# An mLSTM decoder step: gate rows by chunk and head, one empty step ahead of the first gate products, and decode state steps in program order

## The chip, the cores and the metric

The kernel runs on one core of one Trainium2 chip. A core has five engines with queues of their own: TensorE (PE, with its weight loads PEld), VectorE (DVE), ScalarE (ACT), GpSimd (POOL) and SyncE (SP). Each works its own instructions strictly in order and waits on the others through semaphores. The metric is the device time of one execution in microseconds (us).

## What is computed

One layer of a hybrid decoder works on a prompt of 1024 tokens and on 8 single decode tokens. Of the reference, what matters here is the mLSTM gate arithmetic, chunk by chunk (128 tokens, 8 chunks, 4 heads), with `ig` the input gate and `lf` the log forget gate:

```python
b = jnp.cumsum(lf, axis=1).transpose(0, 2, 1)
...
g = b + m[:, :, None]
m_t = jnp.maximum(g, jnp.max(D, axis=-1))
...
ginter = jnp.exp(g - m_t)
...
decay = jnp.exp(b[:, :, -1:] - b + igh - mL[:, :, None])
carry_scale = jnp.exp(b[:, :, -1] + m - mL)
```

`m` is the running maximum that is carried from chunk to chunk. The other two parts that the change touches are the gates of the RG-LRU group (two 64 x 64 products per block of channels, a sigmoid each) and, for each decode token and head, the update of the 256 x 256 state `C = f C + k v`, of which `q C` is then taken.

## The kernel before, in words

**The stages.** First the 1024 rows of x are normalised, transposed and split into pieces (to about 95 us). Then 13 units of the input projection follow (`UNITS`, units 1 to 13; unit 0 is done in the first stage). Each unit is seven products, numbered 0 to 6; a product is two parts, and each part is a run of 12 (q, k, x, y, z units) or 24 (v and o units) matmuls in groups of three (lines 64 to 66). I write "product (2,3) after 5" for the place behind the fifth matmul of product 3 of unit 2. After the units come the chunks of the mLSTM with the output projection in between (from about 690 us), and a short end.

**What runs beside the products.** After each part, `pop_bg` runs what has come due: `late` callbacks, then one step of the queue `bg` (two in units 1 and 13), one of `rgq` (RG-LRU), and in every second or third part one of `dcq` (decode state). The steps of `bg` begin with the generator `gates()` (line 567). Each `yield` in it ends a step. After it comes `rd_open`, which gives the gates' memory to the RG-LRU and decode tiles.

**The order on each engine.** The program is traced in the order of this Python code. A list scheduler then sets each engine's order ahead of time: by its own model of times it takes, in order of tracing, the first instruction that it believes ready. So an instruction that is ready early moves forward, and one that is not ready yet is put behind later matmuls. On the chip the order is fixed: if the model was too hopeful, the engine stands and waits. A place in the middle of a part, such as "(2,3) after 5", therefore marks an instruction that the scheduler put where it had just become ready, without slack.

**`gates()` before.** Parameters are loaded and transposed (L591), a chain of small operations on `gx` (128 x 72) makes the log forget gates (L597 to L602). Sixteen transposes (L630) turn gates into rows of [4 heads, 1024 tokens]; DVE copies them (L631), runs two scans over 1024 elements (L635 running maximum, L636 cumulative sum restarted at each chunk by a mask), and five further passes over [4, 1024] (L639, L642, L654, L656; ACT takes L655 and L657). They land in `stk`, four groups of 4 rows at partitions 0, 32, 64 and 96, and eight transposes (L664) turn `stk` back into columns [128, chunk x head].

**RG-LRU halves.** `rg_half(j, b)` is eight steps: `conv1` (L766, L768), `conv2` (L772, ACT copies L776), `lows` (L783, writes the low parts into `xh` and `xl`), `gate_a` and `gate_b` (the gate products L789), `decay`, `scan`, `outs`.

**Decode state.** For each head and token, `token(b)`: ACT scales the state tile `Cb` (L935), DVE adds k v in two halves (L937, with the broadcast row `vbc` that SP loads at L908), POOL stores it (L939). For every second token, two parts later, four small products (L956) read a pair of states. `Cb` has four buffers, loaded by SP at L914.

Of the kernel before, what the change touches and what calls it, by code (L numbers as in the profile page):

```python
# [9 lines left out]
F32 = mybir.dt.float32  # L10
# [7 lines left out]
P = 128  # L18
# [31 lines left out]
def hymba_kernel(  # L50
# [79 lines left out]
    cs_b = const([P, NH, NCH], "cs_b")  # L130
# [440 lines left out]
    def gates():  # L571
# [49 lines left out]
        stq(s_m, dm[0:1])  # L621
        yield

        rows = fp.tile([NH, 2, T], F32, tag="rows0", name="rows0")
        lfr, igr = rows[:, 0, :], rows[:, 1, :]
        for half in range(2):
            for src, dst in ((lf, lfr), (gs, igr)):
                pr = ps("s" if dst is lfr else "qp", [NH, 512])
                for q in range(4):
                    TE.transpose(pr[:, q * P:(q + 1) * P], src[:, half * 4 + q, 0:NH], idF)  # L630
                (A.copy if dst is igr else V.tensor_copy)(dst[:, half * 512:(half + 1) * 512], pr)  # L631
            yield
        rows1 = fp.tile([NH, 2, T], F32, tag="rows1", name="rows1")
        mr, br = rows1[:, 0, :], rows1[:, 1, :]
        V.tensor_tensor_scan(mr, lfr, igr, 0.0, op0=ALU.add, op1=ALU.max)  # L635
        V.tensor_tensor_scan(br, msk, lfr, 0.0, op0=ALU.mult, op1=ALU.add)  # L636
        yield
        al = lfr
        V.tensor_tensor(al, br, mr, op=ALU.subtract)  # L639
        ld(d_alpha, al)  # L640
        stq(p_m[0, 0].rearrange("(h o) -> h o", o=1), mr[:, T - 1:T])
        V.tensor_tensor(br, igr, br, op=ALU.subtract)  # L642
        c3 = lambda t: t.rearrange("p (c l) -> p c l", l=L)
        sm = fp.tile([NH, 3, NCH], F32, tag="gsm", name="gsm")
        mpv, aL, csr = sm[:, 0], sm[:, 1], sm[:, 2]
        G.memset(mpv, 0.0)
        V.tensor_copy(mpv[:, 1:NCH], c3(mr)[:, 0:NCH - 1, L - 1])
        V.tensor_copy(aL, c3(al)[:, :, L - 1])
        V.tensor_tensor(csr, aL, mpv, op=ALU.add)
        A.activation(csr, csr, AF.Exp)  # L650
        ld(d_cs, csr)
        ld(cs_b, d_cs.partition_broadcast(P))
        yield
        V.tensor_tensor(c3(stk[0:4]), c3(al), mpv.unsqueeze(2).to_broadcast([NH, NCH, L]), op=ALU.add)  # L654
        A.copy(stk[32:36], br)  # L655
        V.tensor_tensor(c3(stk[64:68]), c3(br), aL.unsqueeze(2).to_broadcast([NH, NCH, L]), op=ALU.add)  # L656
        A.mul(stk[96:100], mr, -1.0)  # L657
        for _ in range(5):
            yield
        for half in range(2):  # L660
            pk = ps(("s", "qp")[half], [P, 4, P])
            for q in range(4):
                c = half * 4 + q
                TE.transpose(pk[:, q, :], stk[:, c * P:(c + 1) * P], idF)  # L664
            s = slice(half * 4, half * 4 + 4)
            V.tensor_copy(be_t[:, s, :], pk[:, :, 32:36])
            A.activation(gi_t[:, s, :], pk[:, :, 0:4], AF.Exp)
            A.activation(de_t[:, s, :], pk[:, :, 64:68], AF.Exp)
            A.activation(em_t[:, s, :], pk[:, :, 96:100], AF.Exp)
            yield  # L670
# [77 lines left out]
    def rg_half(j, b):  # L748
# [70 lines left out]
        def outs():  # L819
# [96 lines left out]
    def decode_steps(h):  # L916
# [13 lines left out]
        def token(b):  # L930
            i = h * NB + b

            def f():
                vb_, C = ds_.pop(("v", i)), ds_["C", i]
                A.mul(C, C, dGI[:, b, h:h + 1])  # L935
                for kb in range(2):
                    V.scalar_tensor_tensor(C[:, kb, :], vb_, st["kw"][:, kb, b:b + 1], C[:, kb, :],  # L937
                                           op0=ALU.mult, op1=ALU.add)
# [144 lines left out]
    def w_load(n):  # L1083
        if n < 4 * NCH:
            c, h = n // 4, n % 4
            Ws[n] = mx["p"].tile([P, L], F32, tag="W", name="W", bufs=3)
            ld(Ws[n], d_alpha[h:h + 1, c * L:(c + 1) * L].rearrange("o t -> (o t)").partition_broadcast(P))

    sos = {}
    zt = {}  # L1090
# [87 lines left out]
    def m_b(n):  # L1178
# [8 lines left out]
        pv = ps("tr", [P, 258])  # L1187
        mm3(pv, d["ph"], d["pl"], *mx["v"], True, True)
        for kb in range(2):
            V.scalar_tensor_tensor(mx["Cf"][h][:, kb, :], mx["Cf"][h][:, kb, :], cs_b[:, h, c:c + 1], kvs[kb],  # L1190
                                   op0=ALU.mult, op1=ALU.add)
        V.tensor_tensor(hh, pv[:, 0:257], hh, op=ALU.add)
        if c == NCH - 1:
# [394 lines left out]
```

## Time and profile before

| what | us |
| --- | --- |
| three runs | 941.11, 940.55, 938.7 |
| their median | 940.55 |
| the profiled execution | 939.56 |
| its span, first to last instruction | 937.8 |
| TensorE busy in the span | 918.5 |

The profiled execution's time is 1.76 us more than its span, and 0.99 us less than the median of the three runs. How to read the views: a group row gives line, engine, operation, output and inputs, shape, count, then busy us and mean ns, then the idle time of that engine just before and what ended it. A row of the timeline gives start, duration, engine, line, and in brackets the idle time before it with its releaser. Matmuls overlap: their starts are about 0.23 us apart while each lasts 0.39 us. A row of the view of stretches gives busy time and count of each engine, then the granted TensorE clock, the DMA share and GB/s.

### The profile page before, as it was taken

Reading aid. Unit: us, or ns where it says so; the run is one execution under the profiler, and the core shown is the slowest. Engines: PE = TensorE matmul, PEld = TensorE weight load, DVE = VectorE, ACT = ScalarE, POOL = GpSimd, SP = SyncE. Lnnn points to the kernel's source line nnn. Section 1 sums busy time; section 2 is a strip of 40 time slices with the busy share of each in tenths; the row PEclk is TensorE's granted clock in tenths of the full one; section 3 lists DMA queues with packets and bytes.
Section 4 is the critical chain, followed back from the end, with each engine's and each line's share of the span. In section 5 each row is a group of like instructions: output and inputs, shape, how many; then the busy total and the mean of one; then the engine's idle time right before and its main releaser. Section 6 shows DMA issues by size and latency. Waiting matters only on the chain.

```text
span 937.8 us, 15396 instructions
## 1 busy us (share of the span) xinstructions
PE 918.5 (98%) x5350; PEld 760.6 (81%) x5350; DVE 712.1 (76%) x1465; ACT 590.5 (63%) x1054; POOL 145.6 (16%) x259
## 2 busy tenths in 40 slices
PE   9999989999999999999999999999999999999997
PEld 7897767777787987787789898876578888888886
DVE  7775898989798877988797866668857677667654
ACT  7654457778677757778578774465746466456542
POOL 1111112112212122211122211010111000000110
PEclk9999999999999999999999999999999999999999
DMA  6611457356746464545557363435973563565351
GB/s 197 208 41 44 135 157 264 106 177 203 242 145 209 158 207 164 180 128 196 183 196 242 130 197 107 152 115 181 298 228 118 168 189 116 149 188 162 102 102 46
DMA packets 131383, 153.19 MB, mean 163 GB/s; under 512 B 15816, under 2 KB 110056, under 8 KB 131298
## 3 DMA queue, kind: packets, MB, share of 16 engines
q1 hardware_dynamic: 113578, 96.34, 34.0%
q0 software_dynamic: 17728, 55.87, 16.6%
q8 instruction: 42, 0.69, 0.3%
q14 instruction: 35, 0.29, 0.1%
HBM read 100.59 MB, written 51.65 MB: 162 GB/s over the span
## 4 chain that ended last, share of the span: by engine, by line
PE 82%; DVE 6%; DMA 4%; issue 3%; ACT 2%; SPq 1%; POOL 0%; DVEq 0%; ACTq 0%; POOLq 0%
PE ps_o L64 14%; PE ps_o L66 13%; PE ps_o L65 13%; PE ps_kv L64 9%; PE ps_kv L65 9%; PE ps_kv L66 9%; PE ps_tr L236 2%; PE ps_s L1129 2%; DMA oraw<-in_w_out_dram 1%; DVE wl L71 1%; PE ps_qp L956 1%; PE ps_qp L65 1%; PE ps_qp L64 1%; PE ps_qp L66 1%; PE ps_s L1131 1%
## 5 line engine op out<-in xcount | busy, mean ns | idle before, releaser
L70 ACT CAST wh<-raw 128x1024 fp32r<-128x1024 f32 x91 | 95.4, 1049 | 60.9 <-PE ps_o L65 23.9
L71 DVE TENSOR_TENSOR wl<-raw,wh 128x1024 fp32r<-128x1024 f32 x91 | 110.9, 1219 | 27.2 <-ACT wh L70 17.9
L64 PE MATMUL ps_kv<-cb_hi,wh 128*128 128x512 f32 x320 | 128.0, 400 | 2.0 <-ACT wh L70 1.6
L66 PE MATMUL ps_kv<-cb_hi,wl 128*128 128x512 f32 x320 | 125.3, 392 | 0.0
L65 PE MATMUL ps_kv<-cb_lo,wh 128*128 128x512 f32 x320 | 125.2, 391 | 0.0
L64 PE MATMUL ps_o<-cb_hi,wh 128*128 128x512 f32 x240 | 95.1, 396 | 0.5 <-ACT wh L70 0.5
L66 PE MATMUL ps_o<-cb_hi,wl 128*128 128x512 f32 x240 | 93.8, 392 | 0.0
L65 PE MATMUL ps_o<-cb_lo,wh 128*128 128x512 f32 x240 | 93.6, 390 | 0.0
L64 PEld LDWEIGHTS ps_kv<-cb_hi,wh 128*128 128x128 f32 x320 | 60.1, 188 | 23.8 <-issue 3.0
L65 PEld LDWEIGHTS ps_kv<-cb_lo,wh 128*128 128x128 f32 x320 | 60.2, 188 | 13.3 <-issue 1.7
L66 PEld LDWEIGHTS ps_kv<-cb_hi,wl 128*128 128x128 f32 x320 | 60.1, 188 | 13.0
L64 PE MATMUL ps_kv<-wh,cb_hi 128*128 128x256 f32 x192 | 55.4, 288 | 0.0
L64 PEld LDWEIGHTS ps_o<-cb_hi,wh 128*128 128x128 f32 x240 | 45.1, 188 | 12.3 <-issue 2.5
L65 PE MATMUL ps_kv<-wl,cb_hi 128*128 128x256 f32 x192 | 54.3, 283 | 0.0
L66 PE MATMUL ps_kv<-wh,cb_lo 128*128 128x256 f32 x192 | 54.3, 283 | 0.0
L66 PEld LDWEIGHTS ps_o<-cb_hi,wl 128*128 128x128 f32 x240 | 45.1, 188 | 10.6 <-DVE pf L1138 0.8
L64 PE MATMUL ps_o<-wo,rh 128*128 128x512 f32 (+1 forms) x136 | 53.4, 393 | 0.0
L65 PEld LDWEIGHTS ps_o<-cb_lo,wh 128*128 128x128 f32 x240 | 45.1, 188 | 10.0 <-issue 0.8
L64 PE MATMUL ps_o<-wo,mh 128*128 128x512 f32 (+1 forms) x136 | 52.8, 389 | 0.0
L66 PE MATMUL ps_o<-wo,ml 128*128 128x512 f32 (+1 forms) x136 | 51.7, 381 | 0.0
L66 PE MATMUL ps_o<-wo,rl 128*128 128x512 f32 (+1 forms) x136 | 51.7, 381 | 0.0
L65 PE MATMUL ps_o<-wo,rh 128*128 128x512 f32 (+1 forms) x136 | 51.6, 379 | 0.0
(481 smaller groups left out, 2530.4 us busy)
## 6 DMA issues: line engine op xcount, KB each, us to landing
raw<-in_w_in_dram SPq DMA_DIRECT2D x55, 512.0 KB
Cb<-in_state_mlstm_C_dram SPq DMA_DIRECT2D x32, 256.0 KB
out_dram<-Cb POOLq DMA_DIRECT2D x32, 256.0 KB, 4.6
qk<-d_qk SPq DMA_DIRECT2D x32, 256.0 KB
oraw<-in_w_out_dram SPq DMA_DIRECT2D x16, 512.0 KB
d_qk<-s POOLq DMA_DIRECT2D x24, 256.0 KB, 3.9
d_x<-s POOLq DMA_DIRECT2D x16, 256.0 KB, 2.6
zsr<-d_y SPq DMA_DIRECT2D x16, 256.0 KB
```

The lines of the kernel that those rows point to most:

```text
L64: TE.matmul(out, ah, bh, start=first, stop=False, skip_group_check=True)
L65: TE.matmul(out, ah, bl, start=False, stop=False, skip_group_check=True)
L66: TE.matmul(out, al, bh, start=False, stop=last, skip_group_check=True)
L70: A.copy(hi, src)
L71: V.tensor_tensor(lo, src, hi.bitcast(F32), op=ALU.subtract)
L236: TE.matmul(pz[32 * g:32 * g + 32, :], hnd[:, NB * k:NB * k + 32], raws[u, k // 4][:, k % 4, :], start=k < 4, stop=k >= 4, skip_group_chec ...
L956: TE.matmul(pq[32 * g:32 * g + n, 0:256], q, ds_["C", h * NB + bb][:, kb, :], start=b == 1, stop=b == NB - 1, skip_group_check=True)
L1129: TE.matmul(S, qk[:, 2 + kb, :], qk[:, kb, :], start=kb == 0, stop=kb == 1)
L1131: TE.transpose(kn[:, kb * P:(kb + 1) * P], qk[:, 2 + kb, :], idF)
```

## The change

Three edits. In `gates()`, rows are now 32 (chunk and head) by 128 tokens: two transposes instead of sixteen, scans over 128 elements in 32 rows side by side, a small product (`hsel`, `ends`) that brings the chunk ends to [4, 8], an 8-element scan over chunks, a second small product (`mix`) that brings the carried maximum back to 32 rows, the same passes over [32, 128], and one transpose of `stk` instead of eight. The number of yields stays: 15 steps. In `rg_half` an empty step stands ahead of `gate_a` for b = 0 of j = 0 and 1, so all later RG-LRU steps come one, then two parts later. In `token`, the ACT operation and both DVE operations get an order edge behind the instruction traced just before them on their engine: they can no longer move forward past it.

```diff
-    d_alpha = dram.tile([NH, T], F32, name="d_alpha")
-    d_cs = dram.tile([NH, NCH], F32, name="d_cs")
+    d_alpha = dram.tile([NCH * NH, L], F32, name="d_alpha")
+    d_cs = dram.tile([NCH, NH], F32, name="d_cs")
...
-        stk = fp.tile([P, T], F32, tag="stk", name="stk")
-        msk = fp.tile([NH, T], F32, tag="msk", name="msk")
-        G.memset(msk, 1.0)
-        G.memset(msk.rearrange("p (c l) -> p c l", l=L)[:, :, 0:1], 0.0)
-        G.memset(stk, 0.0)
+        stk = fp.tile([P, L], F32, tag="stk", name="stk")
...
+        G.memset(mo, 0.0)
+        G.tensor_copy(igc.rearrange("p (c h) -> p c h", h=NH), gs[:, :, 0:4])
...
-        for half in range(2):
-            for src, dst in ((lf, lfr), (gs, igr)):
-                pr = ps("s" if dst is lfr else "qp", [NH, 512])
-                for q in range(4):
-                    TE.transpose(pr[:, q * P:(q + 1) * P], src[:, half * 4 + q, 0:NH], idF)
-                (A.copy if dst is igr else V.tensor_copy)(dst[:, half * 512:(half + 1) * 512], pr)
-            yield
...
-        V.tensor_tensor_scan(mr, lfr, igr, 0.0, op0=ALU.add, op1=ALU.max)
-        V.tensor_tensor_scan(br, msk, lfr, 0.0, op0=ALU.mult, op1=ALU.add)
+        V.tensor_reduce(hsel, idc.rearrange("p c h -> p h c"), axis=mybir.AxisListType.X, op=ALU.add)
+        V.tensor_reduce(csel, idc, axis=mybir.AxisListType.X, op=ALU.add)
+        yield
+        yield
...
+        TE.transpose(pr[:, 0, :], lg[:, 0:32], idF)
+        TE.transpose(pr[:, 1, :], igc, idF)
+        A.copy(rows[:, 0:2, :], pr)
+        V.tensor_tensor_scan(ml_, lfr, igr, -1e30, op0=ALU.add, op1=ALU.max)
+        V.tensor_tensor_scan(br, ones[0:CH, :], lfr, 0.0, op0=ALU.mult, op1=ALU.add)
...
+        V.tensor_scalar(ends[:, 0], csel, br[:, L - 1:L], None, op0=ALU.mult)
+        V.tensor_scalar(ends[:, 1], csel, ml_[:, L - 1:L], None, op0=ALU.mult)
+        yield
+        yield
+        yield
...
+        TE.matmul(pe.rearrange("p a c -> p (a c)"), hsel, ends.rearrange("p a c -> p (a c)"), start=True, stop=True)
...
+        V.tensor_copy(be, pe)
+        V.tensor_tensor_scan(mo[:, 1:9], be[:, 0], be[:, 1], 0.0, op0=ALU.add, op1=ALU.max)
...
+        V.tensor_tensor(mix, mo[:, 0:8].unsqueeze(2).to_broadcast([NH, NCH, NH]),
+                        idF[0:NH, 0:NH].unsqueeze(1).to_broadcast([NH, NCH, NH]), op=ALU.mult)
+        yield
+        yield
...
+        TE.matmul(pm, mix.rearrange("p c h -> p (c h)"), ones[0:NH, 0:1], start=True, stop=True)
...
+        V.tensor_copy(mi, pm)
+        V.scalar_tensor_tensor(mr, br, mi, ml_, op0=ALU.add, op1=ALU.max)
         V.tensor_tensor(al, br, mr, op=ALU.subtract)
+        V.tensor_tensor(br, igr, br, op=ALU.subtract)
         ld(d_alpha, al)
...
+        A.copy(stk[32:64], br)
+        A.mul(stk[96:128], mr, -1.0)
+        V.tensor_scalar(stk[0:32], al, mi, None, op0=ALU.add)
+        V.tensor_scalar(stk[64:96], br, aL, None, op0=ALU.add)
+        A.activation(mp[:, 1:2], aL, AF.Exp, bias=mi)
...
+        pk = ps("qp", [P, 4, CH])
+        TE.transpose(pk.rearrange("p g n -> p (g n)"), stk, idF)
...
-        return [conv1, conv2, lows, gate_a, gate_b, decay, scan, outs]
+        wait = [lambda: None] * (b == 0 and j < 2)
+        return [conv1, conv2, lows, *wait, gate_a, gate_b, decay, scan, outs]
...
-                A.mul(C, C, dGI[:, b, h:h + 1])
+                tc.keep_in_program_order(A.mul(C, C, dGI[:, b, h:h + 1]))
                 for kb in range(2):
-                    V.scalar_tensor_tensor(C[:, kb, :], vb_, st["kw"][:, kb, b:b + 1], C[:, kb, :],
-                                           op0=ALU.mult, op1=ALU.add)
+                    tc.keep_in_program_order(V.scalar_tensor_tensor(C[:, kb, :], vb_, st["kw"][:, kb, b:b + 1], C[:, kb, :],
+                                                                    op0=ALU.mult, op1=ALU.add))
```

The rest of the diff follows the new layout: the load of `W` reads row n of `d_alpha`, and `cs_b` is indexed by chunk, then head.

**What the built program shows of the order.** On TensorE the two new transposes stand at (1,6) after 2 (the sixteen of before stood in six groups between the first stage and (1,6) after 3), the two small products at (1,6) after 14 and after 18, the `stk` transpose behind (1,6) among the decode products of the next unit's weights (before: eight at (2,0) after 17). The first gate products L789 stand at (2,2) after 24 and (2,3) after 12 (before: (2,3) after 5 and after 6). The later pair that stood at (3,3) after 13 now stands at (3,4) after 12, the end of a part. Of the 16 groups of L956, five are now split, the second state's two products standing further back, in the middle of a part: (4,3) after 18 and 20, (5,5) after 21 and 23, (6,1) after 25 and 28, (8,5) after 17 and 19, (9,1) after 13 and 14; before, all 16 stood together at ends of parts. L789 stands in the middle of a part at (3,0) after 17 and (6,0) after 36, and between decode products behind (5,6). The first products of the mLSTM chunks (L1129) begin at the end of (11,6) instead of (11,5); from product (13,0) on, the order is that of before but for one place. TensorE has 5037 instructions before and 5018 after.

More of the change, by code (lines that the diff above doesn't have):

```diff
@@ L580, in gates @@
         ld(m0b, st_m[0].partition_broadcast(P))
-        stk = fp.tile([P, T], F32, tag="stk", name="stk")
-        msk = fp.tile([NH, T], F32, tag="msk", name="msk")
-        G.memset(msk, 1.0)
-        G.memset(msk.rearrange("p (c l) -> p c l", l=L)[:, :, 0:1], 0.0)
-        G.memset(stk, 0.0)
+        CH = NCH * NH
+        stk = fp.tile([P, L], F32, tag="stk", name="stk")
+        igc = fp.tile([P, CH], F32, tag="igc", name="igc")
+        mo = fp.tile([NH, 12], F32, tag="mo", name="mo")
+        G.memset(mo, 0.0)
+        G.tensor_copy(igc.rearrange("p (c h) -> p c h", h=NH), gs[:, :, 0:4])
+        idc = idF[0:CH, 0:CH].rearrange("p (c h) -> p c h", h=NH)
+        hsel = fp.tile([CH, NH], F32, tag="hsel", name="hsel")
+        csel = fp.tile([CH, NCH], F32, tag="csel", name="csel")
         dgb = fp.tile([P, NB, 8], F32, tag="dgb", name="dgb")
@@ new lines, in gates @@
+        rows = fp.tile([CH, 6, L], F32, tag="rows", name="rows")
+        lfr, igr, ml_, br, mr, al = (rows[:, n, :] for n in range(6))
+        pr = ps("s", [CH, 2, L])
+        TE.transpose(pr[:, 0, :], lg[:, 0:32], idF)
[3 more added lines that the diff above has]
+        V.tensor_tensor_scan(br, ones[0:CH, :], lfr, 0.0, op0=ALU.mult, op1=ALU.add)
+        ends = fp.tile([CH, 2, NCH], F32, tag="ends", name="ends")
@@ new lines, in gates @@
+        V.tensor_scalar(ends[:, 0], csel, br[:, L - 1:L], None, op0=ALU.mult)
[3 more added lines that the diff above has]
+        yield
+        pe = ps("qp", [NH, 2, NCH])
+        TE.matmul(pe.rearrange("p a c -> p (a c)"), hsel, ends.rearrange("p a c -> p (a c)"), start=True, stop=True)
+        be = fp.tile([NH, 2, NCH], F32, tag="be", name="be")
+        V.tensor_copy(be, pe)
+        V.tensor_tensor_scan(mo[:, 1:9], be[:, 0], be[:, 1], 0.0, op0=ALU.add, op1=ALU.max)
@@ new lines, in gates @@
+        mix = fp.tile([NH, NCH, NH], F32, tag="mix", name="mix")
+        V.tensor_tensor(mix, mo[:, 0:8].unsqueeze(2).to_broadcast([NH, NCH, NH]),
+                        idF[0:NH, 0:NH].unsqueeze(1).to_broadcast([NH, NCH, NH]), op=ALU.mult)
+        yield
+        yield
+        pm = ps("s", [CH, 1])
+        TE.matmul(pm, mix.rearrange("p c h -> p (c h)"), ones[0:NH, 0:1], start=True, stop=True)
+        mp = fp.tile([CH, 2], F32, tag="mp", name="mp")
+        mi, aL = mp[:, 0:1], al[:, L - 1:L]
@@ L646, in gates @@
[L646 to L651, printed above, removed]
+        stq(p_m[0, 0].rearrange("(h o) -> h o", o=1), mr[CH - NH:CH, L - 1:L])
+        A.copy(stk[32:64], br)
+        A.mul(stk[96:128], mr, -1.0)
+        V.tensor_scalar(stk[0:32], al, mi, None, op0=ALU.add)
+        V.tensor_scalar(stk[64:96], br, aL, None, op0=ALU.add)
@@ L652, in gates @@
+        A.activation(mp[:, 1:2], aL, AF.Exp, bias=mi)
+        ld(d_cs.rearrange("c h -> (c h)").rearrange("(p o) -> p o", o=1), mp[:, 1:2])
         ld(cs_b, d_cs.partition_broadcast(P))
         yield
[L654 to L670, printed above, removed]
+        yield
@@ L671, in gates @@
+        yield
+        pk = ps("qp", [P, 4, CH])
+        TE.transpose(pk.rearrange("p g n -> p (g n)"), stk, idF)
+        flat = lambda t: t.rearrange("p c h -> p (c h)")
+        V.tensor_copy(flat(be_t), pk[:, 1, :])
+        A.activation(flat(gi_t), pk[:, 0, :], AF.Exp)
+        A.activation(flat(de_t), pk[:, 2, :], AF.Exp)
+        A.activation(flat(em_t), pk[:, 3, :], AF.Exp)
+        yield
         ids = idF.rearrange("p (a g m) -> p a g m", a=2, g=2)
@@ L1086, in w_load @@
             Ws[n] = mx["p"].tile([P, L], F32, tag="W", name="W", bufs=3)
-            ld(Ws[n], d_alpha[h:h + 1, c * L:(c + 1) * L].rearrange("o t -> (o t)").partition_broadcast(P))
+            ld(Ws[n], d_alpha[n:n + 1, :].rearrange("o t -> (o t)").partition_broadcast(P))
     sos = {}
```

14 lines of the change are left out of this document (2 added, 12 removed).

## The prediction

> **What bounds the kernel now.** I read the page first, then TensorE's waits, then the view of stretches around those waits.
>
> ```profile
> span 937.8 us, 15396 instructions
> ...
> PE 918.5 (98%) x5350; PEld 760.6 (81%) x5350; DVE 712.1 (76%) x1465; ACT 590.5 (63%) x1054; POOL 145.6 (16%) x259
> ...
> PE 82%; DVE 6%; DMA 4%; issue 3%; ACT 2%; SPq 1%; POOL 0%; DVEq 0%; ACTq 0%; POOLq 0%
> ```
>
> TensorE works 918.5 of 937.8 us and holds 82% of the chain that ended last. So a change is worth what it takes from TensorE's own work, plus what it takes from or adds to TensorE's 19.3 us of idle time; relief elsewhere counts only through these two. The waits of TensorE, as wait, releaser, us in total, times, longest:
>
> ```profile
> PE ps_tr L1269 <- DMA oraw<-in_w_out_dram: 2.4, 2, 1.4
> PE ps_s L789 <- DVE xh L783: 2.0, 2, 1.5
> PE ps_s L664 <- DVE stk L656: 1.7, 1, 1.7
> PE ps_kv L64 <- ACT wh L70: 1.6, 1, 1.6
> ...
> PE ps_s L630 <- DVE gx L602: 0.3, 1, 0.3
> ```
>
> Three of them belong to what is changed: L630 and L664 to the gates, L789 to the first gate products of the RG-LRU. All three end with DVE. The stretch around the gates, all instructions first, then those on the tile `rows` alone:
>
> ```profile
> 100.00:125.00 25.00, 23.07 (x115) 16.84 (x115) 24.67 (x55) 11.27 (x19) 3.79 (x7) 1.00 0.28 96
> ```
> ```profile
> 100.00:125.00 25.00, 10.70 (x10) 2.10 (x2) 0.53 (x1) 1.00 0.28 96
> ```
>
> DVE (third number of the first row) is busy 24.67 of 25 us: here it is the bound, and TensorE loses 1.93 us. Of this DVE work 10.70 us, ten operations, are passes over [4, 1024] rows.
>
> **The change, part by part.**
>
> *TensorE's own work.* What a group of four transposes costs, and a single one, is read from the starts of the matmuls around them:
>
> ```profile
> 110.92 0.39 PE L66 MATMUL ps_kv<-cb_hi,wl 128*128 128x512 f32 x1
> 111.21 0.60 PE L630 MATMUL ps_s<-idF,gx 128*4 128x128 f32 x4
> 111.57 0.47 PE L64 MATMUL ps_kv<-cb_hi,wh 128*128 128x512 f32 x1
> 111.88 0.39 PE L65 MATMUL ps_kv<-cb_lo,wh 128*128 128x512 f32 x1
> ```
> ```profile
> 80.68 0.40 PE L66 MATMUL ps_kv<-cb_hi,wl 128*128 128x512 f32 x1
> 80.91 0.28 PE L630 MATMUL ps_qp<-idF,gs 128*4 128x128 f32 x1
> 80.94 0.47 PE L64 MATMUL ps_o<-cb_hi,wh 128*128 128x512 f32 x1
> 81.26 0.39 PE L65 MATMUL ps_o<-cb_lo,wh 128*128 128x512 f32 x1
> ```
> ```profile
> 138.24 0.39 PE L65 MATMUL ps_o<-cb_lo,wh 128*128 128x512 f32 x1
> 138.47 0.39 PE L66 MATMUL ps_o<-cb_hi,wl 128*128 128x512 f32 x1
> ```
>
> Two undisturbed matmuls start 0.23 us apart. With four transposes between, two steps take 111.88 - 110.92 = 0.96, so the four cost 0.96 - 0.46 = 0.50; the single one costs 81.26 - 80.68 - 0.46 = 0.12. Sixteen plus eight transposes go: 24/4 x 0.50 = 3.0 us. Five small operations come: two transposes, two small products, one transpose. The trace has no products of those two small shapes; between nothing and 0.50 each I take the single transpose's 0.12, five times 0.6 us. **TensorE's work: -2.4 us** (bounds -3.0 and -0.5). No other engine hides it, since TensorE has no slack in that stretch.
>
> *DVE's work in the gates.* A pass over 1024 elements, a scan over 1024, and a small operation:
>
> ```profile
> 110.05 0.19 DVE L615 TENSOR_TENSOR dgm<-dgm,dgb 128x32 f32<-128x32 f32 x1
> ...
> 113.52 2.28 DVE L635 TENSOR_TENSOR_SCAN rows<-rows 4x1024 f32<-4x1024 f32 x1
> ...
> 120.84 1.21 DVE L642 TENSOR_TENSOR rows<-rows,rows 4x1024 f32<-4x1024 f32 x1
> ```
>
> From 32 to 1024 elements an operation grows from 0.19 to 1.21, so 128 elements take about 0.29; a scan over 128 takes 2.28 / 8 = 0.29 to some 0.4. The new chain has two such scans, five passes of 128 elements and nine tiny operations: two times 0.4, five times 0.29 and nine times 0.19 are 4.0 at most, against 10.70. DVE gets at least 6 us back where it is the bound. [...]
>
> *The waits that go.* L630 and L664 (one row below) and both L789:
>
> ```profile
> 124.72 0.63 PE L664 MATMUL ps_s<-idF,stk 128*128 128x128 f32 x4 [1.67 <-DVE stk L656]
> ...
> 141.53 0.47 PE L789 MATMUL ps_s<-xh,ghi 128*128 128x512 f32 x1 [1.54 <-DVE xh L783]
> ...
> 187.26 0.47 PE L789 MATMUL ps_s<-xh,ghi 128*128 128x512 f32 x1 [0.42 <-DVE xh L783]
> ```
> ```profile
> 129.73 0.46 SPq L712 DMA_DIRECT2D xs<-d_x  x1
> ```
> ```profile
> 133.94 0.54 DVE L766 TENSOR_SCALAR xc<-xs,PT 128x512 f32<-128x512 f32 x1
> ...
> 139.77 0.89 DVE L937 SCALAR_TENSOR_TENSOR Cb<-vbc,kw,Cb 128x256 f32<-128x256 f32 x2 [1.45 <-DMA vbc<-d_dv]
> 140.70 0.69 DVE L783 TENSOR_TENSOR xh<-xc,xh 64x512 fp32r<-64x512 f32 x1
> ```
>
> The 1.54 us has two causes: DVE comes late to the convolution (L766 at 133.94), and then a decode state step stands in front of L783 and waits 1.45 us for its `vbc` row. The change answers both: DVE has 6 us less to do before, and the pinned state step now stands behind L783. What is late next: the load of `xs` (SP, 129.73) stands behind loads into memory that the `stk` transposes free; with `stk` ready some 7 us sooner it moves forward as well. TensorE reaches the place of the first L789, the start of product (2,3), about 2.4 + 1.9 = 4 us sooner than the 138.69 of before, near 135; DVE, 6 us ahead, finishes L783 one to two us before it. Both L789 now stand at ends of parts. **Waits: -(0.27 + 1.67 + 1.54 + 0.42) = -3.9 us** (the 0.27 is the L630 row of the waits).
>
> *The waits that come in the gates.* The new chain crosses between engines four times: two transposes, ACT copy, DVE scans; product, DVE; product, DVE and ACT; transpose. TensorE's three inner places are in the middle of part (1,6), so they have no slack. Behind a TensorE wait stand the matmuls of that product, and nothing hides it. Bounds for each: nothing, and the 1.67 of L664. The nearest is L630, the first hop of the same chain, 0.27; three times, **+0.8 us**. The last transpose stands behind eight decode products, and I give it nothing.
>
> *The pinned decode steps.* The groups they consist of, and the products that read them:
>
> ```profile
> L937 DVE SCALAR_TENSOR_TENSOR Cb<-vbc,kw,Cb 128x256 f32<-128x256 f32 x64 | 28.4, 479 | 13.9 <-DMA vbc<-d_dv 9.2 <-ACT Cb L935 4.5
> ```
> ```profile
> L935 ACT ACTIVATE Cb<-Cb,dGI 128x512 f32<-128x512 f32 x32 | 22.6, 720 | 12.4 <-DMA Cb<-in_state_mlstm_C_dram 12.3
> ```
>
> The number of operations and loads stays. Today DVE stands 9.2 us and ACT 12.3 us in front of state steps that were moved ahead of their loads; pinned, they come later, when `vbc` and `Cb` have landed. That frees DVE and ACT and is worth nothing by itself: TensorE's waits from 200 to 600 us are one row.
>
> ```profile
> PE ps_kv L64 <- ACT s L319: 0.4, 1, 0.4
> ```
>
> The cost: each state is finished later (0.72 for ACT and twice 0.48 for DVE, behind whatever was traced before), the store on POOL and the `Cb` and `vbc` loads on SP come later with it, and five of the sixteen L956 groups now stand where their second state has only just come ready. With the three L789 places in the middle of a part or unit border, eight places without slack are new. Before had three such L789 places behind the gates: one waited 0.42, the others, at (7,0) after 18 and (10,0) after 32, do not appear among the waits. The mean is 0.14; eight times, **+1.1 us** (bounds nothing, and 8 x 1.67 = 13.4).
>
> *The rest.* `par` products three matmuls later, a POOL memset and copies, the store of `d_alpha` and `d_cs` in other shapes, and the chunk products of unit 11 one product later all lie beside TensorE work; the order from (13,0) on is that of before, so I leave the waits of L1269 and L64 (2.4 and 1.6) and the end alone.
>
> **Sum:** 939.56 - 2.4 - 3.9 + 0.8 + 1.1 = 935.2 for an execution like the profiled one. That one was 0.99 below the median of the runs; I forecast a median, so 936.1.
>
> **The rivals.**
>
> 1. *Slower: the second state of a pair is late.* TensorE is in order; at eight new places without slack it could stand as long as it did at L664. Then 939.56 - 2.4 - 3.9 + 0.8 + 13.4 = 947.5, 948.4 as a median. It turns the gain into a loss once the eight waits exceed (2.4 + 3.9 - 0.8) / 8 = 0.7 us on average. For it: DVE is close to full through these units, and two of the four waits for DVE were over 1.5. Against it: outside the gate stretch such places waited 0.42, 0 and 0.
> 2. *The gate chain gives its gain back.* Four hops at 1.67 instead of 0.8 in all: 935.2 + 5.9 = 941.1, 942.1 as a median. For it: the chain is longer in hops than before. Against: each operation in it is 0.2 to 0.4 us instead of 1.2 to 2.3.
> 3. *The change does not do what it says at L789.* If `xs` or ACT's copies set the time of L783 and not DVE, the 2.0 us stay: 937.2, 938.1 as a median.
> 4. *More is won.* With DVE and ACT ahead, the 1.6 us wait for ACT's weight pieces (L64) goes as well and no new wait comes (0.8 + 1.1): 935.2 - 1.9 - 1.6 = 931.7, 932.7 as a median.
>
> **How the numbers follow.** Forecast 936.1 with 0.52; rival 1 in a form that ends slower 0.15; rival 2 0.13; rival 3 0.12; rival 4 0.08. A measurement of this kernel can tell about 0.3%, 2.8 us, from no change: faster means below 937.7. Faster is forecast and rival 4: 0.60. Same is rivals 2 and 3: 0.25. Slower 0.15. The range reaches from just inside rival 4, 932.5, to 941.0, which takes in rival 3, the weaker half of rival 2 and rival 1 near its break-even; it leaves out about 0.2.
>
> **What would show it.** Right: TensorE's busy time about 2 us lower; no waits named L783 or `stk` on TensorE; DVE busy clearly under 24 of 25 us from 100 to 125; DVE's and ACT's waits for `vbc` and `Cb` mostly gone; small TensorE waits at the new small products and at L956. Wrong: TensorE waits at L956 or L789 that add to over 5 us (rival 1), waits over 1 us at each hop of the gates (rival 2), a wait on `xh` whose row names ACT or a load (rival 3), or new waits after 600 us, where I assumed none to move.

## The result, and the profile after

The changed kernel takes 947.45 us (median of 4 runs, 946.82 to 948.19), the kernel before 939.96 (4 runs). The ratio is 1.0074, 95% interval 1.0061 to 1.0088: 7.5 us slower, where 936.1 was forecast.

The page of after, the same three lines as were shown of before:

```profile
span 945.4 us, 15372 instructions
...
PE 927.6 (98%) x5333; PEld 761.1 (80%) x5333; DVE 707.3 (75%) x1468; ACT 586.7 (62%) x1050; POOL 144.6 (15%) x257
...
PE 77%; DVE 8%; DMA 6%; issue 5%; ACT 3%; SPq 1%; POOL 0%; DVEq 0%; ACTq 0%; POOLq 0%
```

TensorE has 17 records fewer, and yet its busy time rose from 918.5 to 927.6. The span grew by 7.6, so TensorE stands idle 1.5 us less than before; it is *busy* 9.1 us longer. Its waits say the same (releaser, us in total, times, longest):

```profile
PE ps_kv L64 <- ACT wh L70: 1.6, 1, 1.6
PE ps_s L888 <- DVE ORow L889: 1.2, 1, 1.2
...
PE ps_s L803 <- DVE xh L797: 0.8, 1, 0.8
PE ps_qp L971 <- DVE Cb L952: 0.5, 2, 0.3
```

(Lines have moved: L803 is the L789 of before, L971 its L956, L950 and L952 its L935 and L937, L888 its L873.) The decode products L971 wait 0.5 us in all. Nothing here is a loss of 7 us. What was forecast of the gates is there; the stretch from 100 to 125 us, all instructions, then those on the tile `rows` alone (there without TensorE columns):

```profile
100.00:125.00 25.00, 24.85 (x122) 18.00 (x121) 21.95 (x73) 11.64 (x24) 4.87 (x12) 1.00 0.33 109
```
```profile
100.00:125.00 25.00, 2.68 (x9) 1.26 (x4) 0.53 (x1) 1.00 0.33 109
```

DVE is no longer full (21.95 of 25 after 24.67), its passes on `rows` shrank from 10.70 to 2.68 us, and TensorE's idle time there fell from 1.93 to 0.15.

To find the loss I laid the starts of the projection matmuls of both kernels beside each other: there are equally many (2688), in the same order but for two matmuls at the border of (4,4) and (4,5), so the n-th of before and of after do the same work. Three of them, the first of products (1,0), (3,5) and (13,1), before and then after:

```profile
74.31 0.50 PE L64 MATMUL ps_kv<-cb_hi,wh 128*128 128x512 f32 x1
...
197.08 0.39 PE L64 MATMUL ps_o<-cb_hi,wh 128*128 128x512 f32 x1
...
626.27 0.50 PE L64 MATMUL ps_o<-cb_hi,wh 128*128 128x512 f32 x1
```
```profile
75.00 0.50 PE L64 MATMUL ps_kv<-cb_hi,wh 128*128 128x512 f32 x1
...
193.01 0.39 PE L64 MATMUL ps_o<-cb_hi,wh 128*128 128x512 f32 x1
...
633.54 0.50 PE L64 MATMUL ps_o<-cb_hi,wh 128*128 128x512 f32 x1
```

After starts 0.7 late, is 4.1 ahead at (3,5) (a gain of 4.8, close to the forecast), and 7.3 behind at (13,1): 11.3 us are lost in between, far from the gates. Product by product, the loss goes in jumps. Five of 0.9 to 1.9 us lie at (4,3), (5,5), (6,1), (8,5) and (9,1), exactly where a group of four decode products is split; another, 1.1, at (5,6), and one of 1.6 at (11,6), with the wait at L888. Other steps up, the largest 1.8 at (9,0), stand in e1 below as well, where no group is split, and are largely undone by steps down. One group of before, standing together, and the split one of after at (4,3):

```profile
231.49 0.39 PE L66 MATMUL ps_kv<-cb_hi,wl 128*128 128x512 f32 x1
231.81 0.61 PE L956 MATMUL ps_qp<-Cb,qsel 128*4 128x256 f32 x8
232.36 0.50 PE L64 MATMUL ps_kv<-cb_hi,wh 128*128 128x512 f32 x1
232.69 0.39 PE L65 MATMUL ps_kv<-cb_lo,wh 128*128 128x512 f32 x1
```
```profile
230.08 0.40 PE L66 MATMUL ps_kv<-cb_hi,wl 128*128 128x512 f32 x1
230.40 0.60 PE L971 MATMUL ps_qp<-Cb,qsel 128*4 128x256 f32 x2
230.93 0.50 PE L64 MATMUL ps_kv<-cb_hi,wh 128*128 128x512 f32 x1
231.26 0.40 PE L65 MATMUL ps_kv<-cb_lo,wh 128*128 128x512 f32 x1
231.59 0.59 PE L971 MATMUL ps_qp<-Cb,qsel 128*4 128x256 f32 x2
232.12 0.50 PE L66 MATMUL ps_kv<-cb_hi,wl 128*128 128x512 f32 x1
232.46 0.39 PE L64 MATMUL ps_kv<-cb_hi,wh 128*128 128x512 f32 x1
```

A product is two records here (96 + 32 in the view below, for 64 products), so x8 is all four products, x2 a single one. They use 4 columns of the array each (128*4 in the rows) and write to partitions 0, 32, 64 and 96. All four together cost 232.69 - 231.49 minus two undisturbed steps of 0.227, that is 0.75 us. A single one costs 231.26 - 230.08 minus the same: 0.73. **Four together cost what one alone costs**, and a group in three pieces costs some 1.4 us more than a whole one.

The single records of the trace show what is in the price. In the whole group the first records of the four products start within 0.02 us of each other (231.81 to 231.83) and their second records 0.216 later; the two records of a single product are 0.216 apart as well. So, as an estimate from these starts, some 0.43 of the 0.73 us is a product's own running time, twice 0.216, which four products spend side by side; about 0.3 is left. It lies in the steps into and out of the product: 0.32 to its first record (230.08 to 230.40), 0.31 from its second to the next matmul (230.93), and 0.33 from that to the one after, each about 0.1 more than the 0.227 or 0.216 of an undisturbed step. It is not the larger part of the price, and what sets it is not shown: the single four-column transpose of the prediction costs 0.12 in all.

The group view (line, tile, shape and count, then busy us and mean ns, then idle us) shows the whole of it, before and then after:

```profile
L236 PE MATMUL ps_tr<-raw,hnd 128*32 128x512 f32 x224 | 28.0, 599 | 0.2
L956 PE MATMUL ps_qp<-Cb,qsel 128*4 128x256 f32 x96 | 7.4, 379 | 0.0
L956 PE MATMUL ps_qp<-Cb,qfirst 128*32 128x256 f32 x32 | 2.6, 391 | 0.0
```
```profile
L236 PE MATMUL ps_tr<-raw,hnd 128*32 128x512 f32 x224 | 29.2, 599 | 0.3 <-ACT ig L753 0.2
L971 PE MATMUL ps_qp<-Cb,qsel 128*4 128x256 f32 x96 | 11.4, 379 | 0.0
L971 PE MATMUL ps_qp<-Cb,qfirst 128*32 128x256 f32 x32 | 5.0, 391 | 0.5 <-DVE Cb L952 0.5
```

Count and mean are the same to the nanosecond; the busy time, which counts overlapping instructions once, rose from 7.4 + 2.6 = 10.0 to 16.4. A mean alone would have hidden it. L236, the products of the next unit's weights with the decode tokens (16 records of 32 columns in a row), grew by 1.2 us, most of it in the same way: at (5,6) two gate products L803 now stand inside one of its groups, behind its second record, and break a set of four (the records of a whole set start within 0.02 us of each other, as the next four do from 298.15 on). That is 1.0 of the 1.2, since the row has 28.2 in e10, where this group is whole. In (1,6) the new transposition of `stk` stands between the two halves of another L236 group, eight records each. No set of four is broken there, and the way from the matmul ahead of the group to the one behind it grew by only 0.47 us (2.17 to 2.64), the transposition included.

### The profile page after: what moved, and what is told of

Its sections match the earlier page's. It is cut to its first block, busy times and chain, and to the rows that moved or that the text cites. A ratio compares the mean times of both kernels' runs of the same rounds, so it can differ in the third digit from the quotient of the medians.

```text
span 945.4 us, 15372 instructions
## 1 busy us (share of the span) xinstructions
PE 927.6 (98%) x5333; PEld 761.1 (80%) x5333; DVE 707.3 (75%) x1468; ACT 586.7 (62%) x1050; POOL 144.6 (15%) x257
## 3 DMA queue, kind: packets, MB, share of 16 engines
q0 software_dynamic: 17728, 55.87, 16.4%
## 4 chain that ended last, share of the span: by engine, by line
PE 77%; DVE 8%; DMA 6%; issue 5%; ACT 3%; SPq 1%; POOL 0%; DVEq 0%; ACTq 0%; POOLq 0%
PE ps_o L66 13%; PE ps_o L64 13%; PE ps_o L65 13%; PE ps_kv L64 8%; PE ps_kv L65 8%; PE ps_kv L66 8%; PE ps_tr L236 2%; PE ps_s L1144 1%; PE ps_qp L971 1%; DVE wl L71 1%; DMA rl<-d_rm 1%; DMA W<-d_alpha 1%; DMA oraw<-in_w_out_dram 1%; PE ps_qp L65 1%; PE ps_qp L64 1%
## 5 line engine op out<-in xcount | busy, mean ns | idle before, releaser
L66 PEld LDWEIGHTS ps_o<-cb_hi,wl 128*128 128x128 f32 x240 | 45.0, 188 | 11.6 <-issue 1.3
```

What stands on the lines that cost most here:

```text
L66: TE.matmul(out, al, bh, start=False, stop=last, skip_group_check=True)
```

## The experiments

Theory: the loss is the split groups, 5 x 1.4 us, made by the order edges. First rival: it is the empty steps, which move every later RG-LRU step. Second: it is the gates themselves. Times are medians, beside those of the kernel before in the same comparison; each ratio is to that kernel. All kernels compute the whole reference.

### One part at a time

**e1: after without the order edges.**

```diff
-                tc.keep_in_program_order(A.mul(C, C, dGI[:, b, h:h + 1]))
+                A.mul(C, C, dGI[:, b, h:h + 1])
...
-                    tc.keep_in_program_order(V.scalar_tensor_tensor(...))
+                    V.scalar_tensor_tensor(...)
```

> The change without its order edges on the decode state steps (gates by 32 rows and the empty step stay). In its built order all 16 groups of L956 stand together again and the group of decode products at the start of unit 6 too. Theory A (a group of four small products that share the array costs 0.75 us when it stands together, and about 0.73 us for each piece when other matmuls stand in between; so every broken group adds 1.45 us): nothing is left of the loss, the gain up to unit 3 (6 us against before) stays: 933 to 936. Theory B (rival 1 as it was forecast: TensorE waits for a late second state): also fast, since nothing is pinned. Theory C (the later RG-LRU steps collide with decode and the order edges are harmless): stays near 947.

Measured 941.66 beside 940.44, ratio 1.0018 (1.0000 to 1.0035). No group is split, and 5.8 us come back. But 933 to 936 was expected: some 6 us or more are still missing, so the split groups are not all of the loss. At (3,5) this kernel is 4.1 ahead, at (10,3) still 3.0, at (13,1) 0.7 behind.

**e2: before, with the edges alone.**

```diff
+                tc.keep_in_program_order(A.mul(C, C, dGI[:, b, h:h + 1]))
...
+                    tc.keep_in_program_order(V.scalar_tensor_tensor(...))
```

> The kernel before with the order edges alone. In its built order three groups of L956 are broken (one in unit 6, one from 10 into 11, one in 11) and no group of decode weights products. Theory A: 3 x 1.45 = 4.4 us slower, 943 to 945.5, with no TensorE waits to speak of at L956. Theory B: the same five-times-late states, waits of TensorE at L956 that add to the loss, about 8 to 12 us slower. Theory C: no difference from before.

Measured 944.73 beside 940.44, ratio 1.0043 (1.0029 to 1.0058), in the middle of what was expected. Three groups are split, and the busy time of the L956 rows with `qsel` is 11.6 after 7.4: 4.2 us, the whole loss (4.3).

**e3: before, with the new gates alone** (all of the change's diff but the lines of `rg_half` and `token`).

> The kernel before with the rewritten gates alone. No group is broken. As the prediction had it: TensorE's work -2.4, waits of L630 and L664 -1.9, new gate waits up to 0.8, the wait of the first L789 shorter (-1) but the 0.42 stays: 934.5 to 937. If the empty step is what removes the wait at the first L789, this kernel keeps 1.5 us of it: 937 to 938.

Measured 940.47 beside 940.44, ratio 0.9998 (0.9986 to 1.0011): nothing is won, where 934.5 to 938 was expected. TensorE's busy time does fall, by 1.8 us to 916.7, but its waits grow:

```profile
PE ps_tr L1283 <- DMA oraw<-in_w_out_dram: 3.6, 3, 1.4
PE ps_s L803 <- DVE xh L797: 3.5, 2, 3.0
```

TensorE comes to the first gate products sooner than DVE, and waits 3.0 us where it waited 1.5 before; for `oraw` it waits 3.6 where it waited 2.4. The empty step shortens the first of these waits (0.8 in after, 1.0 in e8), but e8 below has gates and step and still wins nothing, so the step alone is not what the gates lack.

**e4: before, with the two empty steps alone.**

```diff
-        return [conv1, conv2, lows, gate_a, gate_b, decay, scan, outs]
+        wait = [lambda: None] * (b == 0 and j < 2)
+        return [conv1, conv2, lows, *wait, gate_a, gate_b, decay, scan, outs]
```

> The kernel before with the empty steps alone. The scheduler leaves the first L789 at product (2,3) after 5, so its wait of 1.5 us should stay, and the later wait of 0.42 should go: 939 to 940, no measurable difference, under all theories but C; by C 5 to 7 us slower.

Measured 943.4 beside 940.44, ratio 1.0037 (1.0023 to 1.0052). I had expected 939 to 940: the steps alone cost about 3 us. The prediction counted them only where they help.

### The split groups

**e5: after, with the four products held together.** The second state's products are issued first and the others get an order edge behind them, so a late state delays the group and does not split it.

```diff
-                for g in range(4):
+                for g in (3, 2, 0, 1):
...
-                    TE.matmul(pq[32 * g:32 * g + n, 0:256], ...)
+                    mm = TE.matmul(pq[32 * g:32 * g + n, 0:256], ...)
+                    if g < 3:
+                        tc.keep_in_program_order(mm)
```

> The change with one thing more: the four products of a pair of states are issued in the order second state, first state, each with an order edge behind the one before, so that they stand together where the second state is ready. All order edges on the state steps stay, and the states are as late as in the change. One group of decode weight products (L236, unit 6) is still broken. Theory A (price of broken groups): 5 x 1.45 = 7.3 us come back, 939 to 941.5. Theory B (late states): the whole group now waits for the second state, so nothing comes back or it gets worse: 947 or more.

Measured 940.74 beside 940.67, ratio 1.0008 (0.9995 to 1.0020). 6.7 us of the loss are gone, with all three edits of the change still in. The L971 rows are back at 7.4 and 2.6. Now the waits that rival 1 of the prediction had in mind do appear, but small:

```profile
PE ps_qp L971 <- DVE Cb L952: 2.2, 4, 0.7
```

**e6: before, with all 16 groups issued in three pieces.** No state is late here; only the place in the order is changed.

```diff
-                    late.append(lambda: late.append(products))
+                    products(0, 1)
+                    late.append(lambda: (products(2), late.append(lambda: products(3))))
...
-                for g in range(4):
+                for g in gs:
```

> The kernel before, with nothing pinned and the states as early as before; only the four products of each pair are issued in three pieces: two at once, one a part later, one another part later. All 16 groups are broken, none has to wait for a state. Theory A: 16 x 1.45 = 23 us slower, 960 to 966, with no new waits of TensorE. Theory B: no state is late, so no more than 2 us of difference.

Measured 962.46 beside 940.67, ratio 1.0239 (1.0218 to 1.0260): 21.8 us for 16 groups, 1.36 each. (This order breaks three L236 groups too, whose row grows by 1.1 us, 28.0 to 29.1; without that it is 1.29 each.) The group view:

```profile
L957 PE MATMUL ps_qp<-Cb,qsel 128*4 128x256 f32 x96 | 21.5, 379 | 0.0
L957 PE MATMUL ps_qp<-Cb,qfirst 128*32 128x256 f32 x32 | 8.1, 391 | 0.0
```

10.0 became 29.6 us, again at the same count and mean, and without a wait. e5 and e6 together settle that a split group costs 1.3 to 1.4 us, and that it takes no late state for that.

### What else is in the balance

e5 still holds the whole gain of the gates at unit 3 and has lost it by unit 13. Four kernels look for where.

**e7: e1, with the two halves of the last RG-LRU row transposes in two PSUM tiles**, against the 1.2 us wait at L888.

```diff
-            po = ps("s", [20, 4, P])
+            po = ps(("s", "qp")[half], [20, 4, P])
```

> The changed kernel without its order edges (941.66 beside 940.44 in its own comparison, +1.2), and the two halves of the last RG-LRU row transposes put in two different PSUM tiles, so that the second half need not wait for the copy of the first (that wait was 1.20 us at product (11,6)). Theory A (the empty steps push this step to a place where nothing covers the copy, and that wait is a real part of their price): about 1.2 us goes, the time ends at that of the kernel before, -0.5 to +0.5 us. Theory B (the copy only shows a delay that the next step, the loads of oraw or the chunk products, would show anyway): within 0.4 us of the kernel without edges, that is +0.8 to +1.6 us against the kernel before.

Measured 941.18 beside 940.65, ratio 0.9998 (0.9987 to 1.0009). The L888 wait is gone, and the time lies at the edge of theory A; but in the profiled execution 2.6 us more than in e1 were lost at (4,4), where the order is still that of e1, so the comparison doesn't settle it. The trace shows something else, on ACT. ACT stands in front of a state step that was moved ahead of its load, 5.08 us here and 4.03 in e1, and some 20 us later TensorE waits for an ACT copy, 2.20 and 1.19:

```profile
217.69 0.72 ACT L950 ACTIVATE Cb<-Cb,dGI 128x512 f32<-128x512 f32 x1 [5.08 <-DMA Cb<-in_state_mlstm_C_dram]
```
```profile
237.02 0.62 PE L64 MATMUL ps_kv<-cb_hi,wh 128*128 128x512 f32 x1 [2.20 <-ACT s L319]
```

Between the two ACT stands only twice, 1.11 and 0.74 us, so the one may well delay the other; no run here shows it by itself.

**e8: e7 with one empty step.**

```diff
-        wait = [lambda: None] * (b == 0 and j < 2)
+        wait = [lambda: None] * (b == 0 and j < 1)
```

> The same, with one empty step (only ahead of the first gate products of j = 0) in place of two. Theory A (each empty step has its price, through all RG-LRU steps that come later because of it; two cost about 3 us alone): about half of that comes back while the gain at the first gate products stays, so 1 to 2 us below the run with two steps, -0.5 to -2.5 us against the kernel before. Theory B (the loss after unit 9 comes from DVE and ACT being ahead in the decode state steps, not from the empty steps): the same as with two steps within 0.5 us. If one step is not enough to cover the first low parts, a wait of 1 to 3 us for xh stands at product (2,2) or (2,3), as with the gates alone (3.0).

Measured 940.59 beside 940.65, ratio 0.9991 (0.9977 to 1.0005). 0.6 below e7: between the two theories. The expected wait for `xh` is there too, 1.0 us at the first gate products.

**e9: e8, and the empty step of before ahead of `rg_rows` taken out.**

```diff
-            rgq.extend([rg_final, lambda: None, rg_rows])
+            rgq.extend([rg_final, rg_rows])
```

> As the run before (one empty step, two PSUM tiles), and the empty step that stands ahead of the last RG-LRU row transposes already in the kernel before is taken out, so that these and the chunk products start at the step where they started in the kernel before. Theory A: everything behind unit 11 falls back into the old order, the gain of 3 to 4 us that stands at unit 3 reaches further, -2 to -4 us against the kernel before. Theory B: the time is set by what comes later than unit 11 (loads of oraw, weight pieces), -0.5 to +0.5 us.

Measured 940.81 beside 940.65, ratio 1.0016 (1.0000 to 1.0033). Theory A fails: giving the last transposes their old step back wins nothing.

**e10: after with its edges, and the edits of e5, e7 and e8: products held together, two PSUM tiles, one empty step.**

> The changed kernel with its order edges, the four decode products held together (second state first), one empty step in place of two, and two PSUM tiles for the row transposes. With two empty steps and one PSUM tile it took 940.74 beside 940.67 (+0.1). Theory A (the broken groups were the large loss, the empty steps and the row transposes the small one): another 1 to 2.5 us comes back, -1 to -2.5 us against the kernel before. Theory B (the edges themselves cost, through waits of DVE and ACT in order): +0.0 to +0.5 us, no change.

Measured 936.58 (5 runs, 935.89 to 938.36) beside 940.65, ratio 0.9960 (0.9947 to 0.9973). More than either theory expected, and faster than both kernels of the study. Its TensorE work is that of before, 918.5 us, at a span of 934.5:

```profile
span 934.5 us, 15378 instructions
...
PE 918.5 (98%) x5333; PEld 760.5 (81%) x5333; DVE 703.6 (75%) x1468; ACT 588.3 (63%) x1050; POOL 144.7 (15%) x257
```

e8 and e10 differ only in the edges and the order of the four products. ACT's state steps in e8, then in e10 (busy and mean, then idle time ahead of them and what ended it):

```profile
L950 ACT ACTIVATE Cb<-Cb,dGI 128x512 f32<-128x512 f32 x32 | 22.5, 719 | 18.6 <-DMA Cb<-in_state_mlstm_C_dram 15.6 <-PE ps_o L65 2.9
```
```profile
L950 ACT ACTIVATE Cb<-Cb,dGI 128x512 f32<-128x512 f32 x32 | 23.0, 718 | 0.2
```

15.6 us in which ACT stood for loads are gone, and TensorE's waits for ACT's copy L319, for `xh` and for `oraw` go from 1.3, 1.8 and 1.4 us in e8 to 0.4, 0.9 and nothing.

### The four parts, each undone or alone

**e11: e10 with the second empty step back** (`j < 2` again).

> The changed kernel with its edges, the decode products held together, two PSUM tiles for the row transposes and both empty steps; it differs from the run that took 936.58 (-4.1 beside 940.65) only in the second empty step, and from the one that took 940.74 only in the PSUM tiles. Theory A (each empty step has a price of about 1.5 us): -1.5 to -3 us against the kernel before. Theory B (the single PSUM tile cost it, 1 to 2 us at product (11,6), and the second step costs nothing): -3.5 to -4.5. Theory C (all of it is the second empty step, which in the built order also breaks the group of decode weight products at (5,6) into three): -0.5 to +0.5.

Measured 940.82 beside 940.53, ratio 1.0001 (0.9983 to 1.0019). Theory C: the second step costs the 4.2 us, the PSUM tiles nothing (e5 took 940.74). The trace shows how: the span is 3.7 longer than that of e10; the L971 waits are back, and L236 is split again:

```profile
PE ps_qp L971 <- DVE Cb L952: 2.7, 4, 0.8
```
```profile
L236 PE MATMUL ps_tr<-raw,hnd 128*32 128x512 f32 x224 | 29.2, 599 | 0.3 <-ACT ig L753 0.2
```

2.7 of waits, and 1.0 of L236 (29.2, where e10 has 28.2), are those 3.7 us. The empty step puts RG-LRU steps and state steps into other parts beside each other. In e10 they fall so that no group has to wait for a state step; a step further they fall badly. The 4.2 us are a price in this company only: e7 and e8 differ in the same step, without the edges, and there it is 0.6, within the intervals of both.

**e12: before, with edges and products held together only.**

> The kernel before with the order edges on the decode state steps and the four products of a pair held together (second state first): no new gates, no empty step. With the edges alone it took 944.73 (+4.1). Theory A (only the broken groups cost; the edges themselves are worth nothing by themselves, as the prediction had it): -0.5 to +1 us. Theory B (without edges ACT and DVE stand 12.3 and 9.2 us at loads, and part of it reaches TensorE; held together, the edges are a gain): -1 to -3 us.

Measured 941.83 beside 940.53, ratio 1.0016 (1.0001 to 1.0031), 0.3 past the end of theory A: by themselves the edges win nothing. There too L956 waits for `Cb`, 1.9 us in four places.

**e13: e10 with the four products in their usual order, not held together.** Five groups are split.

> The fastest kernel so far (936.58) with one part undone: the four decode products issued in their usual order and not held together. In the built order five of the sixteen groups are then broken into two or three pieces with other matmuls between ((4,0-1), (4,3), (6,1), (8,5), (9,1)). Theory A (a broken group costs 0.7 for each piece beyond the first, 1.36 us when it is in three): five times 1.36, some 943.4, +2 to +3.5 us against the kernel before. Theory B (the broken groups cost only with the two empty steps): 936 to 938.

Measured 944.65 beside 940.53, ratio 1.0041 (1.0026 to 1.0055), 8.1 us above e10 where theory A made it 6.8, and past the upper end of what was expected. The L971 rows:

```profile
L971 PE MATMUL ps_qp<-Cb,qsel 128*4 128x256 f32 x96 | 12.2, 379 | 0.4 <-DVE Cb L952 0.4
L971 PE MATMUL ps_qp<-Cb,qfirst 128*32 128x256 f32 x32 | 4.0, 391 | 0.0
```

They have 16.2 us where e10 has 10.0. Of the 8.2 us by which the span grew, TensorE's busy time makes 6.8 (918.5 to 925.3), 6.2 of it in these rows. The other 1.4 are waits: 3.2 us for `oraw` near the end are new beside e10, and others are shorter.

**e14: e10 with the gates of before.**

> The fastest kernel so far (936.58) with the gates of the kernel before: order edges, products held together, one empty step, two PSUM tiles. Theory A (the new gates are worth the 2.4 us of TensorE work and the 1.9 us of waits at L630 and L664 that the prediction gave them, and with one empty step the rest stays): 3.5 to 4.5 us slower than that kernel, -0.5 to +0.5 against the kernel before. Theory B (as in the run with the gates alone, their gain is given back at the next place that DVE or ACT sets, and the edges are what won): the same as the fastest within 1 us, -3 to -4.

Measured 940.49 beside 940.53, ratio 1.0008 (0.9993 to 1.0022). Theory A: the new gates are worth 3.9 us once everything else is in order.

The balance goes from before to after in steps, each from a pair of kernels that differ in what the first column names:

| step | pair | us |
| --- | --- | --- |
| new gates | e14 to e10 | -3.9 |
| edges held together, one empty step, two PSUM tiles | before to e14 | 0.0 |
| second empty step | e10 to e11 | +4.2 |
| one PSUM tile again | e11 to e5 | -0.1 |
| groups split | e5 to after | +6.7 |
| sum | | +6.9 |
| measured | before to after | +7.5 |

Each pair starts at the kernel where another ends, so the sum has to close, and that it does confirms nothing; the 0.6 us between sum and result are the medians of before, 940.53 in the one comparison and 939.96 in the other. The sizes hold for this order of steps: by themselves the new gates win nothing (e3), and the second empty step without the edges costs 0.6 (e7 and e8).

## Why the prediction was wrong

- **TensorE's own work, -2.4, and the waits that go, -3.9.** The mechanism was right and the size nearly: with the hops (+0.8) they make 5.5, and a gain of 4.8 stands at (3,5). For the gates alone the forecast makes 2.4 + 1.9 - 0.8 = 3.5, and e14 to e10 gives 3.9; TensorE's busy time falls by 1.8 in that pair and in e3. The first gate products still wait 0.8 where I gave them nothing.
- **Waits that come in the gates, +0.8.** Too much: only the first transposes show up, with 0.2 (e10 and e11), the small products not at all.
- **The pinned decode steps, +1.1: the step that failed.** I saw that five groups were split and priced each at 0.14 us of waiting. The waits are 0.5 in all, so that price was even too high. What I left out is that four products that share the array cost no more than one (0.75 us and 0.73), so that every piece of a split group is paid like the whole: some 1.36 us a group (e6), 6.7 in all (e5 to after). The trace of before has it: x8 in 0.61 us (231.81), where one record has a mean of 379 ns. I took "TensorE's work" to be a count of instructions added and removed, and did not price those that only moved.
- **"Frees DVE and ACT and is worth nothing by itself."** It does free them: ahead of the state steps ACT stands 0.3 us after 12.4, DVE 6.0 after 13.9. Worth nothing is true alone (e12: +1.3), false in company: between e8 and e10 the edges, with the products held together, are worth 4.0 us, most likely because TensorE, now 4 us ahead, meets an ACT that still stands for loads; e12 lacks the gates and the empty step both, so this is argued and not shown.
- **The rest, "all lie beside TensorE work": the second failed step.** The second empty step costs 4.2 us with the edges (e11), by waits of the decode products and a split L236 group. I had named the L236 place, between decode products behind (5,6), and counted it as a wait of 0.14. The two failed steps together make 10.9 of the 11.4 us between forecast and result. That e10, which has neither (and two PSUM tiles), comes out at 936.58, so close to the 936.1 of the forecast, is partly luck: its gain needs the edges, to which I gave no worth.
- **The rivals.** Rival 1 gave 947.5 for the profiled execution, and its median, 948.4, is within 1 us of the result; but its mechanism, TensorE waiting at L956, is not what happened, so the near number is luck. The wait exists (2.2 us in e5, 2.7 in e11), at a fifth of the price that I gave it. Rival 3's outcome, nothing won at the first gate products, is what e3 shows without the empty step (3.0 us of wait), though there TensorE waits for DVE, and rival 3 had the load or ACT set the time.
- **What would show it.** "TensorE's busy time about 2 us lower" was the check that decided: it is 9.1 higher, and that line of the page points at moved work and not at a wait. The waits after 600 us, where I assumed none to move, did move (1.1 us for `rl` is new, `oraw` has 1.5 less), with little in balance.

## What to carry to other kernels

Where small products run side by side in the array, as the four here do (0.75 us together, 0.73 one alone), price the piece and not the product: look for the group's busy time beside count times mean, and keep each group whole when an order is changed, even if it has to wait for its last operand (e5: 6.7 us back, for waits of 2.2). An order edge on a producer on DVE or ACT can move its consumers on TensorE (here it split five of 16 groups, three in e2), so read the new order there first. And a shift by one step in a fixed rotation of side work need not be free, so try each phase: here the first empty step, with the edges, cost nothing that showed, and the second 4.2 us, which without the edges was 0.6.

## What the runs showed that I had not expected

In e7 the wait of 2.20 us shown above was followed by a stretch in which projection matmuls started 0.43 us apart, where 0.23 is usual. The view of stretches (busy time of PE, PEld, DVE, ACT and POOL, then the granted clock):

```profile
237.00:238.00 1.00, 0.98 (x3) 0.77 (x4) 0.97 (x2) 0.98 (x2) 0.00 (x0) 0.63 0.81 311
238.00:239.00 1.00, 1.00 (x4) 0.81 (x3) 0.97 (x2) 0.97 (x3) 0.00 (x0) 0.50 0.96 206
239.00:240.00 1.00, 1.00 (x4) 0.71 (x4) 0.94 (x3) 0.48 (x1) 0.54 (x1) 0.50 0.79 209
240.00:241.00 1.00, 1.00 (x5) 0.83 (x3) 1.00 (x4) 0.00 (x0) 0.00 (x0) 0.67 1.07 304
```

```profile
240.77 0.39 PE L64 MATMUL ps_kv<-cb_hi,wh 128*128 128x512 f32 x1
```

The granted clock was about halved for some 3 us (0.50 in the two middle rows). From the row at 237.02 to this one are nine steps in 3.75 us, where undisturbed steps of 0.227 take 2.04: 1.7 us more, on top of the wait of 2.2. I found no such stretch behind the wait of 3.0 us in e3 (mean granted clock 0.998, in e7 0.997), nor behind the shorter waits of the other runs. So the wait and the stretch behind it cost 3.9 us together here; no run shows whether the one brought the other, or what decides it.
